# Token-block sums on VectorE alone, 1.6 setup steps per group, input matrices held for the later pairs

## The chip, the cores and the metric

The kernel runs on one core of a Trainium2 chip. The metric is the device time of one launch in microseconds (us). A core has TensorE (PE in the profile; its weight loads are PEld), VectorE (DVE), ScalarE (ACT), GpSimd (POOL) and SyncE (SP, which here issues all DMAs). Each engine runs its own instructions strictly in the order in which they stand, and waits on semaphores for the others.

## The reference

One layer of a hybrid encoder block over 768 tokens (512 of one request, 256 of another), width 1024, in float32:

```python
h = rms_norm(x, g_ffn1_pre)
x = x + 0.5 * rms_norm(swiglu(h, w_ffn1_gate, w_ffn1_up, w_ffn1_down), g_ffn1_post)
z = rms_norm(x, g_mix_pre) @ w_in          # -> u, q_c, kv_c, k_rope
y_ssm = rms_norm(s5_mixer(u, fwd, bwd, d_skip, w_glu, b_glu), g_ssm_out)
y_att = rms_norm(mla_mixer(q_c, kv_c, k_rope, g_q, w_uq, g_kv, w_ukv), g_att_out)
x = x + rms_norm(concat([y_ssm, y_att]) @ w_out, g_mix_post)
x = x + 0.5 * rms_norm(swiglu(rms_norm(x, g_ffn2_pre), w_ffn2_gate, w_ffn2_up, w_ffn2_down), g_ffn2_post)
```

`swiglu(x, g, u, d)` is `(silu(x @ g) * (x @ u)) @ d` with 2816 inner columns. The state-space mixer `s5_mixer` is a linear recurrence of 32 groups of 64 complex states in both directions. Its matrices depend on the weights alone, so the kernel works them out while the first feed-forward block (FFN1) runs.

## The kernel before

Every float32 operand of a matmul is split into a high and a low part (`split`, lines 97 to 99: a cast on ACT at L98, then a subtraction on DVE at L99), and each product is three matmuls: high by high (L117, L125), high by low (L118, L126), low by high (L119, L127). So ACT and DVE have to prepare every weight tile `w` before PE can use it.

A feed-forward block walks over 11 pairs of 256 inner columns (`ffn`). FFN1 does pairs 0 to 2 in the plain way (`plain`): eight groups of 24 matmuls of 384 columns each, four for gate and four for up, each group for one half of the tokens. From pair 3 on it uses a Strassen-Winograd form (`wino`) with seven products instead of eight. The form needs sums and differences of the four blocks B00, B01, B10, B11 of the normed tokens. `combos` makes them: four full blocks F (L266), three differences L280, L283, L285 and a fourth, L286, and then the split parts T1 to T4 (high on ACT at L271, low at L272). Each of these is one instruction over 128x1536 elements. In the kernel before, the sums of B11 and B10 (both L266), L286 and the low part T4l are on POOL, and the others on DVE. In the program's text `combos` is run beside the down products of pair 2 (FFN1) or of pair 0 (FFN2, which has one plain pair).

The down product of a pair (`down(q)`) is 12 groups of six matmuls of 512 columns (tile ps_d). In the first down product ACT copies each result to `acc` (L451); in the later ones DVE adds it (L453). A group can only start when one of two to four banks of ps_d has been read.

The state-space setup (`ssm_setup`, a generator of 99 steps) runs in the background of FFN1. After each group the call `behind(background, PACE[...])` adds a credit and runs as many steps as the credit allows, so that their instructions are written behind those of the group. The numbers of steps per group are 3.0 in pair 0, 1.15 in the other plain pairs and their down products, and 0.75 in the down products of the later pairs. The steps are, in order: 28 that build powers and factors; the way back (`ssm_back`, 22 steps), which transposes C (ps_c, L698) and then eight times makes two matrices on DVE (three instructions of 128x576 each, L679, L681 and L682, tiles ssm_w and ssm_t), multiplies them on PE (ps_k, L718, 16 small matmuls for each of the eight), and reads the two result banks on DVE (L726, L727) and ACT (L728, L729) into ssm_kf; then 48 steps for the 16 input matrices dM (L679 to L682 again, now of 128x512, on DVE; a transpose ps_m on PE; a copy on ACT; a DMA). The tiles ps_k have two banks, so one of the eight blocks can start on PE only when ssm_kf of the block before it has been read out.

The order within an engine is made by a scheduler from the text's order and the data each instruction needs; what it made of the two kernels is shown below where it matters.

Of the kernel before, what the change touches and what calls it, by code (L numbers as in the profile page):

```python
# [11 lines left out]
ALU = mybir.AluOpType  # L12
# [26 lines left out]
    return slice(HALF * i, HALF * i + HALF)  # L39


PACE = (3.0, 1.15, 0.75)
BACK = 27
WOUT = (35, 36, 37, 38)
AHEAD = 3
# [3 lines left out]
class Kernel:  # L49
    N6, N4, N2 = 20, 16, 4  # L50

    def __init__(self, tc, A, outs):
        self.tc, self.nc, self.A, self.outs = tc, tc.nc, A, outs
        self.credit, self.latest = 0, {}
        self.turns, self.free = [0, 0], False


    def s6(self, name, shape, dtype=F32):
# [202 lines left out]
    def combos(self, bl, out):  # L261

        def whole(kh, nh, eng):
            f = self.s6(f"F{kh}{nh}", [4, HALF])
            hi, lo = bl["B"][kh, nh]
            eng.tensor_tensor(f, hi.bitcast(F32), lo.bitcast(F32), op=ALU.add)  # L266
            return f

        def parts(name, src, eng):
            out[name] = h, l = tuple(self.s6(name + z, [4, HALF], F32R) for z in "hl")  # L270
            self.nc.scalar.copy(h, src)  # L271
            eng.tensor_tensor(l, src, h.bitcast(F32), op=ALU.subtract)  # L272

        dve, pool = self.nc.vector, self.nc.gpsimd
        b11 = whole(0, 0, dve)
        b22 = whole(1, 1, pool)
        yield
        b12 = whole(0, 1, dve)
        yield
        dve.tensor_tensor(b11, b12, b11, op=ALU.subtract)  # L280
        b21 = whole(1, 0, pool)
        yield
        dve.tensor_tensor(b12, b22, b12, op=ALU.subtract)  # L283
        yield
        dve.tensor_tensor(b22, b22, b11, op=ALU.subtract)  # L285
        pool.tensor_tensor(b21, b22, b21, op=ALU.subtract)  # L286
        yield
        parts("T2", b22, dve)
        yield
        parts("T1", b11, dve)  # L290
        yield
        parts("T3", b12, dve)
        parts("T4", b21, pool)
        yield

    def group(self, last, calls):
# [25 lines left out]
    def ffn(self, bl, wnames, way_out, n_plain, feed, lead, background=iter(()), read=lambda nh: None):  # L322
# [31 lines left out]
        def plain(q):  # L354
# [16 lines left out]
            for nh in range(2):  # L371
                for m in "gu":
                    for i in range(2):
                        if q == 0 and nh == 0:
                            next(feed, None)
                        with self.in_order() if q == 0 and nh == 0 else nullcontext():
                            if (m, i) not in ops:
                                get(m, i)
                            ps = self.gu([128, HALF])
                            for kh in range(2):  # L380
                                self.prod(ps, ops[m, i][kh], B[kh, nh], kh == 0, kh == 1)
                            if q == 0 and nh == 0 and m == "g":
                                get("u", i)
                            gate_done(hs, i, nh, ps) if m == "g" else up_done(hs, q, i, nh, ps)
                        if q or nh:
                            self.behind(background, PACE[1 if q else 0])

        def wino(m, q, T, hs, U):
# [69 lines left out]
        def down(q, side=background):  # L458
            product = row_of([q])[1]
            for t in range(NTILE):  # L460
                for dh in range(2):
                    product(t, dh, self.dn)()
                    if side is background:
                        self.behind(side, PACE[2 if q >= n_plain else 1])
                if side is not background:
                    next(side, None)
# [57 lines left out]
    def ssm_setup(self):  # L524
# [132 lines left out]
                yield  # L657
        yield from self.ssm_back(tB, PX)
        del tB, tC, tD, sm, PW, q, PX
        for b in range(16):  # L660
            w = self.s6("ssm_w", [3, 512])
            self.product(w[:, 0], w[:, 1], Bm, QW, 2 * b, 8)
# [620 lines left out]
```

## Time and profile before

| | |
|---|---|
| three runs | 1495.70, 1499.86, 1505.25 us; median 1499.86 us |
| profiled execution | 1495.48 us; its span from first to last instruction 1493.7 us |
| PE busy | 1410.8 us, 94% of the span |
| PEld, DVE, ACT, POOL busy | 87%, 67%, 38%, 18% |
| granted TensorE clock, mean | 0.981 |

All numbers of rows below come from the profiled execution; times in them count from the start of its span. A row of the timeline gives start, duration, engine, source line, operation, output and inputs, how often the instruction was repeated in a row, and in brackets the idle time of the engine before it with what ended it. A matmul is shown longer than it holds the engine, since matmuls overlap: the distance from one start to the next is what one costs. The same holds, by 0.05 to 0.08 us, for instructions on DVE.

### The profile page before, as it was taken

The numbers are of one execution on the slowest core, as the hardware profiler recorded it, in microseconds if no ns is written. First come the engines' busy times: TensorE is split into PE (matmuls) and PEld (weight loads), VectorE is DVE, ScalarE is ACT, GpSimd is POOL, SyncE is SP. The second block draws the span as 40 slices with busy tenths as digits, with TensorE's granted clock in tenths as the row PEclk, the third lists the DMA queues.
The fourth block names the chain that finished last, engine by engine and source line by source line (L and its number), as shares of the span: only waits on it lengthen the run. The fifth ranks groups of instructions, "written<-read, shape, count | busy, mean of one in ns | idle before, by whom it ended". The sixth has DMA issues, their size and how long they took to land. (4 is left out here: it accounts for less than half of the span.)

```text
span 1493.7 us, 20350 instructions
## 1 busy us (share of the span) xinstructions
PE 1410.8 (94%) x7868; PEld 1293.5 (87%) x7868; DVE 1006.9 (67%) x1614; ACT 574.5 (38%) x1085; POOL 263.4 (18%) x413
## 2 busy tenths in 40 slices
PE   6999779999999998899998899799999999999997
PEld 6989559999999997899877888598999999999995
DVE  5566898778887676624265545798777667776664
ACT  5331224223333242434764654346333222332231
POOL 1300110000000004203998112432000000000004
PEclk9999989999999999999999899899999999999999
DMA  9403412323213143553106334332221212212224
GB/s 240 88 14 99 147 36 87 104 71 106 79 64 99 57 130 95 167 163 98 22 14 165 90 102 148 120 104 81 71 71 57 85 57 73 83 53 75 72 84 113
DMA packets 116066, 137.51 MB, mean 92 GB/s; under 512 B 31745, under 2 KB 96641, under 8 KB 115969
## 3 DMA queue, kind: packets, MB, share of 16 engines
q1 hardware_dynamic: 115968, 136.21, 30.6%
q8 instruction: 62, 1.02, 0.3%
q14 instruction: 36, 0.29, 0.1%
HBM read 113.44 MB, written 21.95 MB: 91 GB/s over the span
## 5 line engine op out<-in xcount | busy, mean ns | idle before, releaser
L98 ACT CAST w<-raw 128x512 fp32r<-128x512 f32 (+3 forms) x327 | 219.5, 694 | 274.4 <-DVE raw L397 58.9
L99 DVE TENSOR_TENSOR w<-raw,w 128x512 fp32r<-128x512 f32 (+3 forms) x327 | 265.3, 823 | 56.7 <-ACT w L98 47.2
L453 DVE TENSOR_TENSOR acc<-acc,ps_d 128x512 f32<-128x512 f32 x216 | 146.5, 684 | 117.1 <-PE ps_d L127 117.0
L125 PE MATMUL ps_d<-w,hid 128*128 128x512 f32 x528 | 210.3, 399 | 11.4 <-DVE acc L453 6.2
L126 PE MATMUL ps_d<-w,hid 128*128 128x512 f32 x528 | 209.3, 396 | 2.0 <-DVE w L99 2.0
L127 PE MATMUL ps_d<-w,hid 128*128 128x512 f32 x528 | 208.1, 396 | 0.2 <-DVE hid L99 0.2
L1189 POOL TENSOR_SCALAR g<-g 128x1024 f32<-128x1024 f32 x2 | 5.6, 2778 | 738.6 <-DMA g<-in_g_ffn_post 414.4
L125 PEld LDWEIGHTS ps_d<-w,hid 128*128 128x128 f32 x528 | 100.3, 190 | 33.7 <-DVE acc L453 8.8
L127 PEld LDWEIGHTS ps_d<-w,hid 128*128 128x128 f32 x528 | 100.4, 190 | 22.3 <-DVE hid L99 0.6
L126 PEld LDWEIGHTS ps_d<-w,hid 128*128 128x128 f32 x528 | 100.4, 190 | 20.0 <-DVE w L99 2.5
L98 ACT CAST hid<-hs 128x384 fp32r<-128x384 f32 x88 | 44.3, 512 | 90.7 <-DVE hs L348 90.6
L400 ACT COPY U<-pa 128x384 f32<-128x384 f32 x36 | 17.2, 479 | 116.4 <-PE pa L119 111.4
L344 ACT ACTIVATE hs<-hs 128x384 f32<-128x384 f32 x54 | 27.7, 523 | 88.8 <-DVE hs L430 76.5
L99 DVE TENSOR_TENSOR hid<-hs,hid 128x384 fp32r<-128x384 f32 x88 | 47.9, 551 | 8.6 <-ACT hid L98 8.6
L118 PE MATMUL pb<-T2l,w 128*128 128x384 f32 x144 | 49.3, 342 | 2.9 <-DVE T2l L272 2.9
L119 PE MATMUL pa<-B00h,w 128*128 128x384 f32 x144 | 48.4, 336 | 0.8 <-DVE w L99 0.8
L119 PE MATMUL pb<-T2h,w 128*128 128x384 f32 x144 | 49.2, 342 | 0.0
L117 PE MATMUL pb<-T2h,w 128*128 128x384 f32 x144 | 48.9, 340 | 0.0
L994 DVE TENSOR_REDUCE mx<-ps_s 128x1 f32<-128x512 f32 (+1 forms) x40 | 27.2, 685 | 32.0 <-PE ps_s L991 32.0
L117 PE MATMUL pa<-B00h,w 128*128 128x384 f32 x144 | 48.3, 336 | 0.0
L117 PE MATMUL pe<-B11h,w 128*128 128x384 f32 x144 | 48.3, 336 | 0.0
L118 PE MATMUL pa<-B00l,w 128*128 128x384 f32 x144 | 48.3, 335 | 0.0
(367 smaller groups left out, 3769.8 us busy)
## 6 DMA issues: line engine op xcount, KB each, us to landing
raw<-in_w_ffn_gate SPq DMA_DIRECT2D x44, 512.0 KB, 4.6
raw<-in_w_ffn_up SPq DMA_DIRECT2D x44, 512.0 KB, 4.7
raw<-in_w_ffn_down SPq DMA_DIRECT2D x44, 512.0 KB, 3.9
x<-in_x_prompt SPq DMA_DIRECT2D x16, 256.0 KB, 8.0
dO<-ssm_w SPq DMA_DIRECT2D x16, 256.0 KB, 3.7
dM<-ssm_w SPq DMA_DIRECT2D x16, 256.0 KB, 2.0
raw<-dM SPq DMA_DIRECT2D x8, 512.0 KB, 5.7
raw<-dO SPq DMA_DIRECT2D x8, 512.0 KB, 3.8
```

The costliest lines, as they stand in the source:

```text
L98: self.nc.scalar.copy(hi, src)
L99: (eng or self.nc.vector).tensor_tensor(lo, src, hi.bitcast(F32), op=ALU.subtract)
L117: self.nc.tensor.matmul(ps, A[0][:, k, :], B[0][:, k, :], start=first, stop=False, skip_group_check=True)
L118: self.nc.tensor.matmul(ps, A[0][:, k, :], B[1][:, k, :], start=False, stop=False, skip_group_check=True)
L119: self.nc.tensor.matmul(ps, A[1][:, k, :], B[0][:, k, :], start=False, stop=stop and k == 3, skip_group_check=True)
L125: self.nc.tensor.matmul(ps, lh, rh, start=i == 0, stop=False)
L126: self.nc.tensor.matmul(ps, lh, rl, start=False, stop=False)
L127: self.nc.tensor.matmul(ps, ll, rh, start=False, stop=last)
L344: nc.scalar.activation(hs[:, i, half(nh)], ps, AF.Silu)
L400: nc.scalar.copy(U2, pa)
L453: tt(acc[:, t, sl], acc[:, t, sl], ps, op=ALU.add)
L994: nc.vector.tensor_reduce(m, ps, axis=AX.X, op=ALU.max)
```

## The change

Three edits. In `PACE` the second number goes from 1.15 to 1.6, so a plain group (and a group of a plain pair's down product) takes 1.6 setup steps with it. A flag `halfway` is set when `ssm_back` has ended; from then on only the down products of the later pairs run setup steps, so that of the dM matrices one is begun in the plain pairs and the rest comes with the later pairs. And in `combos` all instructions that were on POOL are on DVE.

```diff
-PACE = (3.0, 1.15, 0.75)
+PACE = (3.0, 1.6, 0.75)
...
-        self.turns, self.free = [0, 0], False
+        self.turns, self.free, self.halfway = [0, 0], False, False
...
-        dve, pool = self.nc.vector, self.nc.gpsimd
+        dve = self.nc.vector
         b11 = whole(0, 0, dve)
-        b22 = whole(1, 1, pool)
+        b22 = whole(1, 1, dve)
...
-        b21 = whole(1, 0, pool)
+        b21 = whole(1, 0, dve)
...
-        pool.tensor_tensor(b21, b22, b21, op=ALU.subtract)
+        dve.tensor_tensor(b21, b22, b21, op=ALU.subtract)
...
-        parts("T4", b21, pool)
+        parts("T4", b21, dve)
...
-                        if q or nh:
+                        if (q or nh) and not self.halfway:
                             self.behind(background, PACE[1 if q else 0])
...
-                    if side is background:
+                    if side is background and (q >= n_plain or not self.halfway):
                         self.behind(side, PACE[2 if q >= n_plain else 1])
...
         yield from self.ssm_back(tB, PX)
         del tB, tC, tD, sm, PW, q, PX
+        self.halfway = True
+        yield
```

After the change all lines behind the constructor of the class stand up to two lines lower (L679 is L681, L718 is L720, L726 is L728).

**PE, between the first down product and pair 2.** Before: the second and third rows of the down product's last group, one of the eight ps_k blocks (16 matmuls in the order, which the trace counts as 32), and then the gate products of pair 2 (ps from B00).

```order
L126 MATMUL ps_d<-w,hid 128x512
L127 MATMUL ps_d<-w,hid 128x512
L718 MATMUL ps_k<-ssm_w,ssm_b 32x128 x16
L117 MATMUL ps<-B00h,w 128x384
L118 MATMUL ps<-B00l,w 128x384
L117 MATMUL ps<-B00h,w 128x384
```

Now, at the same place:

```order
L126 MATMUL ps_d<-w,hid 128x512
L127 MATMUL ps_d<-w,hid 128x512
L720 MATMUL ps_k<-ssm_w,ssm_b 32x128 x64
L117 MATMUL ps<-B00h,w 128x384
L118 MATMUL ps<-B00l,w 128x384
L720 MATMUL ps_k<-ssm_w,ssm_b 32x128 x8
L117 MATMUL ps<-B00h,w 128x384
L118 MATMUL ps<-B00l,w 128x384
L117 MATMUL ps<-B00h,w 128x384
L118 MATMUL ps<-B00l,w 128x384
L720 MATMUL ps_k<-ssm_w,ssm_b 32x128 x8
L119 MATMUL ps<-B00h,w 128x384
```

Five of the eight ps_k blocks (64 and twice 8 matmuls) now stand ahead of the first low-part product (L119) of pair 2, where one stood. A first block stands further up, inside the down product (not shown), and ps_c stands behind 24 matmuls of the down product where it stood behind 48.

**DVE, the same place.** Before: the low parts `w` of pair 2's weights (L99) stand among the matrices of the way back.

```order
L681 TENSOR_TENSOR ssm_t<-ssm_ct,ssm_d 128x2x2x144
L99 TENSOR_TENSOR w<-raw,w 128x512 x2
L726 SCALAR_TENSOR_TENSOR ssm_kf<-mask,dsk,ps_k 128x16
L681 TENSOR_TENSOR ssm_t<-ssm_ct,ssm_d 128x2x2x144 x2
L682 TENSOR_TENSOR ssm_w<-ssm_w,ssm_t 128x576
L99 TENSOR_TENSOR w<-raw,w 128x512 x2
```

Now, where the first `w` of pair 2 stands:

```order
L729 TENSOR_TENSOR ssm_kf<-ssm_kf,ps_k 128x16
L684 TENSOR_TENSOR ssm_w<-ssm_w,ssm_t 128x576 x2
L728 SCALAR_TENSOR_TENSOR ssm_kf<-mask,dsk,ps_k 128x16
L681 TENSOR_TENSOR ssm_w<-ssm_ct,ssm_d 128x576
L683 TENSOR_TENSOR ssm_t<-ssm_ct,ssm_d 128x2x2x144
L681 TENSOR_TENSOR ssm_w<-ssm_ct,ssm_d 128x576
L683 TENSOR_TENSOR ssm_t<-ssm_ct,ssm_d 128x2x2x144
L729 TENSOR_TENSOR ssm_kf<-ssm_kf,ps_k 128x16
L99 TENSOR_TENSOR w<-raw,w 128x512 x2
L683 TENSOR_TENSOR ssm_t<-ssm_ct,ssm_d 128x2x2x144
L684 TENSOR_TENSOR ssm_w<-ssm_w,ssm_t 128x576
L99 TENSOR_TENSOR w<-raw,w 128x512 x2
```

From the first matrix to that first `w` DVE now has 40 instructions of 128x576 and ten small ones of ssm_kf; before, it had 11 of 128x576 there.

**DVE, the block sums of FFN1.** Before: the two sums that DVE had stand among the additions to `acc` of the down products of pairs 1 and 2, behind a part of a third dM matrix.

```order
L453 TENSOR_TENSOR acc<-acc,ps_d 128x512
L679 TENSOR_TENSOR ssm_w<-ssm_a 128x512
L681 TENSOR_TENSOR ssm_w<-ssm_a,ssm_q 128x2x2x128
L266 TENSOR_TENSOR F_1689<-B00h,B00l 128x1536
L266 TENSOR_TENSOR F_1709<-B01h,B01l 128x1536
L99 TENSOR_TENSOR w<-raw,w 128x512
L453 TENSOR_TENSOR acc<-acc,ps_d 128x512 x2
```

Now all four stand ahead of the first addition to `acc`, behind the only dM matrix that is begun in the plain pairs:

```order
L681 TENSOR_TENSOR ssm_w<-ssm_a 128x512
L683 TENSOR_TENSOR ssm_w<-ssm_a,ssm_q 128x2x2x128
L266 TENSOR_TENSOR F_1667<-B00h,B00l 128x1536
L266 TENSOR_TENSOR F_1669<-B11h,B11l 128x1536
L266 TENSOR_TENSOR F_1687<-B01h,B01l 128x1536
L266 TENSOR_TENSOR F_1706<-B10h,B10l 128x1536
L396 TENSOR_TENSOR raw<-raw 128x4x128 x2
L684 TENSOR_TENSOR ssm_w<-ssm_w 128x512
L99 TENSOR_TENSOR w<-raw,w 128x1024
L280 TENSOR_TENSOR F_1667<-F_1687,F_1667 128x1536
L348 TENSOR_TENSOR hs<-hs,ps 128x384
```

The four sums moved up, ahead of the last `hs` of pair 2 (L348), while PE still has pair 2's products to do. On PE the 24 groups of the two down products, which stood mostly ahead of pair 3's products, now alternate with them; behind pair 3 both orders hold the same work.

## Rows read from the trace of the kernel before

**Rows 1.** The page: busy share in 40 slices of 37.3 us, in tenths.

```profile
PE   6999779999999998899998899799999999999997
DVE  5566898778887676624265545798777667776664
```

**Rows 2.** Busy time (times instructions) by stage: PE, PEld, DVE, ACT, POOL, PEclk, DMA, GB/s.

```profile
91.06:150.00 58.94, 55.82 (x428) 49.86 (x428) 35.83 (x65) 18.11 (x38) 0.00 (x0) 0.97 0.29 72
150.00:225.00 75.00, 54.90 (x299) 41.77 (x299) 69.35 (x87) 20.61 (x33) 14.91 (x4) 0.91 0.30 91
225.00:244.94 19.94, 19.94 (x114) 19.53 (x114) 15.85 (x26) 8.12 (x15) 0.00 (x0) 1.00 0.42 137
...
244.94:545.00 300.06, 300.06 (x1607) 280.89 (x1607) 234.88 (x389) 106.21 (x188) 0.00 (x0) 1.00 0.24 77
...
1000.00:1025.00 25.00, 22.53 (x111) 19.66 (x110) 24.31 (x26) 14.15 (x22) 8.79 (x2) 1.00 0.14 43
```

**Rows 3.** Timeline of PE: what matmuls cost, and where the stage stalls.

```profile
99.94 0.39 PE L125 MATMUL ps_d<-w,hid 128*128 128x512 f32 x1
100.62 0.39 PE L125 MATMUL ps_d<-w,hid 128*128 128x512 f32 x1
101.99 1.03 PE L698 MATMUL ps_c<-ident,craw 128*128 128x128 f32 x8
112.25 0.69 PE L119 MATMUL ps<-B00h,w 128*128 128x384 f32 x1 [0.93 <-DVE w L99]
115.62 0.37 PE L117 MATMUL ps<-B10h,w 128*128 128x384 f32 x1
117.75 0.33 PE L117 MATMUL ps<-B00h,w 128*128 128x384 f32 x1
118.27 0.33 PE L117 MATMUL ps<-B00h,w 128*128 128x384 f32 x1
167.84 0.64 PE L718 MATMUL ps_k<-ssm_w,ssm_b 64*32 64x128 f32 x16 [2.71 <-ACT ssm_kf L729]
202.48 0.79 PE L125 MATMUL ps_d<-w,hid 128*128 128x512 f32 x1 [4.68 <-DVE acc L453]
218.15 0.69 PE L118 MATMUL pb<-T2l,w 128*128 128x384 f32 x1 [2.85 <-DVE T2l L272]
244.94 0.33 PE L117 MATMUL pa<-B00h,w 128*128 128x384 f32 x1
```

**Rows 4.** Timeline of DVE: the way back, weights, additions, block sums.

```profile
103.78 0.76 DVE L679 TENSOR_TENSOR ssm_w<-ssm_ct,ssm_d 128x576 f32<-128x576 f32 x1 [10.07 <-ACT ssm_ct L699]
105.92 0.75 DVE L679 TENSOR_TENSOR ssm_w<-ssm_ct,ssm_d 128x576 f32<-128x576 f32 x1
114.87 1.28 DVE L99 TENSOR_TENSOR w<-raw,w 128x512 fp32r<-128x512 f32 x2
197.21 1.75 DVE L266 TENSOR_TENSOR F<-B00h,B00l 128x1536 f32<-128x1536 f32 x1
198.88 1.75 DVE L266 TENSOR_TENSOR F<-B01h,B01l 128x1536 f32<-128x1536 f32 x1
201.15 1.27 DVE L453 TENSOR_TENSOR acc<-acc,ps_d 128x512 f32<-128x512 f32 x2
```

**Rows 5.** Timeline of POOL and DVE: the same kinds of instruction beside POOL and alone.

```profile
173.99 3.51 POOL L266 TENSOR_TENSOR F<-B10h,B10l 128x1536 f32<-128x1536 f32 x1 [1.75 <-DVE w L99]
...
174.59 3.46 DVE L395 TENSOR_TENSOR s<-raw 128x512 f32<-128x512 f32 x1
179.77 0.68 DVE L395 TENSOR_TENSOR s<-raw 128x512 f32<-128x512 f32 x1
...
1007.78 3.52 POOL L286 TENSOR_TENSOR F<-F,F 128x1536 f32<-128x1536 f32 x1 [12.38 <-DVE F L285]
...
1008.03 3.82 DVE L99 TENSOR_TENSOR w<-raw,w 128x512 fp32r<-128x512 f32 x1
...
1017.42 0.50 PE L125 MATMUL ps_d<-w,hid 128*128 128x512 f32 x1 [2.47 <-ACT acc L451]
```

## The prediction

> **What bounds the kernel now.** I read the page's slices first: PE is at 9 tenths nearly everywhere, and among the four dips below 8 tenths lies one in slices 5 and 6 (187 to 224 us), where DVE stands at 8 and 7 [rows 1]. So the kernel is bound by PE, and only time in which PE stands still or runs slowly can be won. Then I cut FFN1 into stages [rows 2]. From 91.06 us (first down product) to 150 PE idles 3.1 us of 58.9. From 150 to 225 it idles 20.1 us of 75, and DVE is busy 69.35 of them: there PE waits for DVE. From 225 PE is never idle, up to 545. The granted clock is 0.97 and 0.91 in the first two stages and 1.00 in the other two; 1.00 is 2.4 GHz, and one step below is 1.2 GHz, so a mean of 0.91 over 75 us is 13.5 us at the lower level, of which half is lost. That is the price of the stalls on top of the idle time. The timeline names the stalls: an addition to acc that comes late on DVE (4.68 us at 202.48), the low part of T2 (2.85 at 218.15), a ps_k block behind ssm_kf (2.71 at 167.84) [rows 3]. A row to hold the change against: at 244.94 PE begins the first product of pair 4's gate [rows 3]. Up to there both orders put the same work on PE, but for two of the dM transposes ps_m, which now come later (of the order of 0.55 us each, by ps_c's eight in 1.03 [rows 3]).
>
> **Prices.** Three matmuls of a down group start every 100.62 - 99.94 = 0.68 us, so a group of six costs 1.36 and 24 of them 32.6. Three of 384 columns cost 118.27 - 117.75 = 0.52, so pair 2's 192 cost 33.3 and the 156 of pair 3 up to pair 4's first cost 27.0 [rows 3]. A matrix of the way back (three instructions) costs DVE 105.92 - 103.78 = 2.14, or 0.71 each; a w of 512 columns 0.60 to 0.64 (two in 1.28); an addition the same (two in 1.27); an instruction of 1536 columns 198.88 - 197.21 = 1.67 [rows 4]. So the work of PE from 91.06 to 244.94 is 36 groups 49.0, ps_c 1.0, eight ps_k blocks of 0.65 5.2, pair 2 33.3, pair 3 27.0, two ps_m 1.1: 116.6 of 153.9. The other 37.3 are idle time, slow clock and restarts; this is what the change can win at most in FFN1.
>
> **Edit 1, 1.6 steps: the way back comes earlier and in one block.** ps_c moves up by 24 matmuls, 5.4 us, from 101.99 to 96.6. DVE had then waited 10.07 us for it [rows 3, 4]. It can't use all 5.4: part of the factor work now stands behind the last hs of pair 1, and I let the first matrix start at 100 instead of 103.78. Ahead of the first w of pair 2 stand 40 instructions of the way back, 40 x 0.71 = 28.4, and ten small ones of ssm_kf, 1.5 together by an estimate of 0.15 each (their rows are not costed singly): DVE reaches that w at 130, and PE has its low part at 130.7. Meanwhile PE has eight groups left in the down product, 10.9 us from 97.6, about 1 us of waiting for the first block of ps_k, and six blocks of 0.65: it runs dry at about 111 and idles some 16.5 us up to 130.7. This is the new wait, and all of pair 2 is queued behind it, on PE in the same order. It takes the place of the 3.1 us before 150. From 130.7: 190 matmuls, 33.0, two blocks 1.3, and 1.7 because PE restarts slowly (before, after its stalls, ten matmuls took 115.62 - 112.25 = 3.4 us, twice their 1.7 [rows 3]). PE ends pair 2 at 166.7.
>
> What this buys: the way back is done when pair 2 begins, and through these 36 us DVE has only pair 2's own work, two of the eight blocks and the four sums F, which need nothing of pair 2. I take the two down products and pair 3, 32.6 + 27.0 = 59.6 us of PE, and walk the two orders against each other by these prices: PE waits for an addition behind a 1.67 us instruction at five places and for T3's low part once, 0.2 to 1.6 us each, together 4.5. Pair 4 begins at 166.7 + 59.6 + 4.5 = 230.8, which is 14.1 earlier than 244.94; some 24 of the 37.3 stay lost. Bounds: if each handover ps_k to ssm_kf to the next ps_k takes 1.5 us more in five rounds (a wait of 2.71 for one stands in [rows 3]), the block costs 7.5 more; if the first matrix starts at 98.4, 1.6 less. The 4.5 lie between 0 and 10.2, which the three stalls at 167.84, 202.48 and 218.15 alone cost now [rows 3]; I am near the low end, since the F rows now stand in time that PE fills with pair 2.
>
> **Edit 2, dM held.** Two dM matrices with their products (3 x 0.64 = 1.9 us of DVE each) go from the plain pairs to the later ones: their DVE time is in the sum above, since they are out of the walked rows. In the later pairs PE is busy 300.06 of 300.06 us and DVE 234.9 [rows 2]; the rate there stays 0.75 steps a group, and 47 steps need 63 of 72 groups, so none is left for the end. Their price is the PE time alone, 2 x 0.55 = 1.1 us. If DVE were no cover there, it would be 3.8 more. The dM transfers also stay behind the copies in SP's queue; weights behind them are loaded a pair ahead. Zero for that, at most 1.
>
> **Edit 3, no POOL.** DVE takes four more instructions of 1.67 in each feed-forward block, 6.7 us. But it doesn't lose that: beside a POOL instruction of 3.51 us a DVE instruction took 3.46 that takes 0.68 alone, and beside one of 3.52 another took 3.82 [rows 5]. These two lost 2.78 and 3.14 us (the w of 512 columns 0.68 alone, too). I take 2.5 for each of the four, 10 in each block, so DVE gains about 3 there; the bounds are 2 and 3.2 each. In FFN1 this is in the walk, which uses the prices of instructions alone. In FFN2 PE loses only 2.47 us near 1017, an addition on ACT that is late behind a weight DVE had not finished [rows 2, 5]; I take 2 of it, between 0 and 2.5.
>
> The Trainium skill, SBUF — State Buffer, section "SBUF: two separate sides", calls the port pair of the two engines an exclusive lock: who comes second is blocked for the whole instruction. The rows agree in kind (3.46 beside 3.51), but by the rule DVE would lose all of POOL's 14.9 us in FFN1 [rows 2], where the two rows lose 2.8 and 3.1 of 3.5; the sum would come out up to 5 us lower, 1479.
>
> **Sum.** FFN1: 14.1 - 1.1 = 13.0, less 2 for a further dip of the clock among the short waits at 175 to 190, as an estimate (in the stage from 150 the clock costs 6.7 us): 11. FFN2: 2. Together 13, against the execution's own 1495.48: 1482.5. The median of the runs, 1499.86, lies 4.4 above that execution, so a run at the median would come to 1487; I say 1484.
>
> **Rivals.**
> *The wait only moves (no change).* The 16.5 us on PE are real, and of the 20.1 us that PE idles from 150 to 225 [rows 2] more than 9 stay, because T2 to T4 still have to be made between additions. Then FFN1 gives 0 to 6, the total 2 to 8: 1490. For it: DVE's work up to pair 4 hardly shrinks, and DVE was busy 69 of 75 us. Against it: it was idle 23 of 58.9 us before 150, and that is the time now used.
> *Slower.* The handovers of the five blocks are as long as before, 7.5 us more, and DVE comes to pair 2's end so late that all 20.1 us stay: 16.5 + 7.5 - 3.1 = 21 lost, 1.1 for dM: 1495.5 + 22 - 2 = 1515. It is slower as soon as more than about 12 of the 20.1 stay: the block costs 13.4 net, and each idle us of that stage brings half as much again in slow clock and restarts. Against it: four F sums and both L395 stand ahead of the first addition now.
> *More.* The five short waits vanish (4.5), the clock stays at 2.4 GHz behind 134 (2), FFN2 gives 2.5: 13 + 7 = 20, 1476.
> *Clock.* PE idles long at 111 to 131; should it stay at 1.2 GHz through pair 2's first half, that is 8 us more: 1491. The rows have it back after 3.4 us, so this is in the first rival's share.
> The Trainium skill, TensorE: Matmul & The Clock Gate, Part 1, has the array's clock fall to half when it is idle and come back under load. The row from 112.25 shows that for a short stall; no run here shows it for 16 us.
>
> **How the numbers follow.** My case, a gain of 8 to 17 us: 0.52. The wait moves: 0.27. More: 0.14. Slower: 0.07. The range 1474 to 1497 holds my case with both ends of its unknown terms, most of the second, and half of the third, with some 4 us of spread between runs. About 1% (15 us) is what a measurement of this kernel can tell from no change. Faster by over that: "more" and the top two fifths of mine, 0.34; slower 0.07; the rest, 0.59, is within it.
>
> **What would show it.** ps_c near 96.6 and the first matrix near 100; a PE gap of some 16 us ending near 131 on DVE's first w of pair 2; PE idle below 6 us from there to pair 4, which begins near 231; no DVE row above 3 us; PE full in the later pairs, DVE about 4 us busier there; no wait of 2.47 in FFN2. Wrong if the gap is over 22 us, or if waits for acc and T2 over 10 us remain behind it.

## The result, and the profile after

Four runs of the changed kernel took 1478.53 to 1480.35 us, median 1479.79; four runs of the kernel before, beside them, 1495.70 to 1505.87, median 1502.55. The ratio is 0.9871, with a 95% interval of 0.9848 to 0.9894: 1.29% faster. A second set gave 1477.67 against 1496.79, 0.9867 (0.9847 to 0.9886). The profiled execution took 1479.79 us, 15.7 less than the 1495.48 of before; the prediction's sum for this pair was 13.0.

The page of the changed kernel, busy tenths in 40 slices (here of 36.95 us), answers to [rows 1]:

```profile
PE   6998999999999997999997999799999999999997
DVE  5578977877878666525164635797687666776764
```

The dip of slices 5 and 6 is gone from PE's row; one digit of 8 stands in slice 4, where the way back of the state-space setup now lies. By stage (columns as in [rows 2]), from the first down product at 92.07 us on, and in FFN2:

```profile
92.07:150.00 57.93, 50.79 (x439) 40.54 (x439) 49.09 (x86) 19.43 (x43) 0.00 (x0) 0.85 0.53 143
150.00:225.00 75.00, 72.29 (x367) 64.99 (x366) 63.78 (x84) 22.83 (x36) 0.00 (x0) 1.00 0.18 58
...
229.82:530.00 300.18, 300.18 (x1612) 281.38 (x1612) 237.09 (x398) 108.67 (x191) 0.00 (x0) 1.00 0.26 81
...
985.00:1010.00 25.00, 25.00 (x126) 22.56 (x126) 24.72 (x28) 15.25 (x23) 0.00 (x0) 1.00 0.16 43
```

Ahead of 150 us PE now idles 7.1 us where it idled 3.1, at a mean clock of 0.85 where it was 0.97. From 150 to 225 it idles 2.7 where it idled 20.1, and the clock is 1.00 where it was 0.91. The later pairs are full as before, and in FFN2 the idle 2.5 us are gone. The timeline of PE shows the places, answering to [rows 3]:

```profile
97.56 1.03 PE L700 MATMUL ps_c<-ident,craw 128*128 128x128 f32 x8
114.67 0.64 PE L720 MATMUL ps_k<-ssm_w,ssm_b 64*32 64x128 f32 x16 [1.82 <-ACT ssm_kf L730]
116.76 1.08 PE L720 MATMUL ps_k<-ssm_w,ssm_b 64*32 64x128 f32 x16 [1.45 <-ACT ssm_kf L731]
124.61 1.08 PE L720 MATMUL ps_k<-ssm_w,ssm_b 64*32 64x128 f32 x16 [1.68 <-ACT ssm_kf L731]
125.61 0.69 PE L117 MATMUL ps<-B00h,w 128*128 128x384 f32 x1
130.14 0.69 PE L119 MATMUL ps<-B00h,w 128*128 128x384 f32 x1
165.70 0.39 PE L125 MATMUL ps_d<-w,hid 128*128 128x512 f32 x1
180.91 0.50 PE L125 MATMUL ps_d<-w,hid 128*128 128x512 f32 x1 [1.21 <-DVE acc L453]
188.91 0.44 PE L118 MATMUL pc<-T3l,w 128*128 128x384 f32 x1 [1.21 <-DVE T3l L272]
229.82 0.33 PE L117 MATMUL pa<-B00h,w 128*128 128x384 f32 x1
```

The idle time ahead of 126 lies in the handovers between one ps_k block and the next (a block can start when ssm_kf of an earlier one has been read out). Pair 2 begins at 125.61 with its high parts and gets its first low part at 130.14; it ends at 165.70, where the next down product starts. Behind it two waits of 1.21 us remain for an addition and for T3's low part. Pair 4 begins at 229.82, where it began at 244.94: 15.12 us earlier. On DVE, answering to [rows 4]:

```profile
100.25 0.76 DVE L681 TENSOR_TENSOR ssm_w<-ssm_ct,ssm_d 128x576 f32<-128x576 f32 x1 [0.26 <-ACT ssm_ct L701]
128.41 1.30 DVE L99 TENSOR_TENSOR w<-raw,w 128x512 fp32r<-128x512 f32 x2
154.63 1.75 DVE L266 TENSOR_TENSOR F<-B00h,B00l 128x1536 f32<-128x1536 f32 x1
159.63 1.76 DVE L266 TENSOR_TENSOR F<-B10h,B10l 128x1536 f32<-128x1536 f32 x1
```

The 40 instructions of the way back and the small ones among them run from 100.25 to 128.41 without a hole, and the four block sums from 154.63 on, while PE still works on pair 2.

### The profile page after: what moved, and what is told of

Its sections match the earlier page's. It is cut to its first block, busy times and chain, and to the rows that moved or that the text cites. A ratio compares the mean times of both kernels' runs of the same rounds, so it can differ in the third digit from the quotient of the medians.

```text
span 1478.0 us, 20330 instructions
## 1 busy us (share of the span) xinstructions
PE 1410.6 (95%) x7868; PEld 1295.5 (88%) x7868; DVE 994.9 (67%) x1622; ACT 575.1 (39%) x1085; POOL 229.5 (16%) x405
## 5 line engine op out<-in xcount | busy, mean ns | idle before, releaser
L99 DVE TENSOR_TENSOR w<-raw,w 128x512 fp32r<-128x512 f32 (+3 forms) x327 | 252.4, 783 | 58.3 <-ACT w L98 48.2
L395 DVE TENSOR_TENSOR s<-raw 128x512 f32<-128x512 f32 x36 | 24.8, 692 | 42.7 <-DMA raw<-in_w_ffn_up 35.6
L99 DVE TENSOR_TENSOR hid<-hs,hid 128x384 fp32r<-128x384 f32 x88 | 48.8, 556 | 7.0 <-ACT hid L98 7.0
L118 PE MATMUL pc<-T3l,w 128*128 128x384 f32 x144 | 48.2, 335 | 1.2 <-DVE T3l L272 1.2
L119 PE MATMUL pb<-T2h,w 128*128 128x384 f32 x144 | 48.3, 336 | 0.0
L119 PE MATMUL pa<-B00h,w 128*128 128x384 f32 x144 | 48.3, 336 | 0.0
```

The costliest lines, as they stand in the source:

```text
L99: (eng or self.nc.vector).tensor_tensor(lo, src, hi.bitcast(F32), op=ALU.subtract)
L118: self.nc.tensor.matmul(ps, A[0][:, k, :], B[1][:, k, :], start=False, stop=False, skip_group_check=True)
L119: self.nc.tensor.matmul(ps, A[1][:, k, :], B[0][:, k, :], start=False, stop=stop and k == 3, skip_group_check=True)
L395: tt(s1, a21, a22, op=ALU.add)
```

## The experiments

Each kernel is read at three distances in its profile, all between starts on PE: from the first down product to pair 4's gate (FFN1's critical stretch); from pair 1 to pair 2 of FFN2 (where `combos` runs there); and from the first attention product ps_s to pair 1 of FFN2, where all kernels have the same code. Ratios are to the kernel before, in the same set of runs, with 95% intervals. Of the eight combinations of the three edits two were not run: the steps with the sums but without the hold, and the hold with the sums but without the steps.

| kernel | down product to pair 4 | pair 1 to 2, FFN2 | ps_s to pair 1, FFN2 | median, us | ratio |
|---|---|---|---|---|---|
| before, first and second profile | 153.88, 153.60 | 40.92, 41.35 | 268.3, 267.4 | 1496.8 to 1502.6 | 1 |
| 1.6 steps alone | 170.48 | 41.37 | 267.9 | 1511.98 | 1.0107 (1.0088 to 1.0125) |
| hold alone | 147.72 | 42.49 | 272.8 | 1497.29 | 0.9986 (0.9968 to 1.0004) |
| sums on DVE alone | 151.47 | 38.18 | 267.4 | 1493.77 | 0.9971 (0.9958 to 0.9984) |
| 1.6 steps and hold | 136.70 | 41.37 | 269.9 | 1481.20 | 0.9896 (0.9881 to 0.9910) |
| same, sums on DVE in FFN2 only | 136.68 | 38.19 | 272.5 | 1481.15 | 0.9887 (0.9863 to 0.9911) |
| changed (all three), two profiles | 137.75, 137.22 | 38.18, 38.19 | 268.5, 268.5 | 1479.79, 1477.67 | 0.9871, 0.9867 |
| changed, 1.4 steps | 140.73 | 38.18 | 268.0 | 1483.98 | 0.9895 (0.9871 to 0.9918) |
| changed, 4.5 and 1.6 | 130.81* | 38.18 | 272.7 | 1481.73 | 0.9890 (0.9861 to 0.9920) |
| changed, 5.0 and 1.45 | 131.36* | 38.18 | 272.3 | 1479.50 | 0.9875 (0.9854 to 0.9897) |
| changed, 5.0 and 1.6 | 129.29 | 38.19 | 273.1 | 1476.21 | 0.9830 (0.9798 to 0.9862) |
| changed, 7.0 and 1.0 | 120.68* | 38.19 | 268.4 | 1485.73 | 0.9908 (0.9884 to 0.9932) |

(*) Not the same work: in these three, 204 matmuls ps_d stand ahead of pair 4's begin, in all others 216. The other 12, two groups of 1.36 us, come later, so 2.7 us of these distances are only moved.

**One edit at a time: 1.6 steps alone.**

```diff
-PACE = (3.0, 1.15, 0.75)
+PACE = (3.0, 1.6, 0.75)
```

> Edit 1 without edits 2 and 3: 1.6 steps per plain group, dM not held, POOL kept. In the order about ten more dM matrices come ahead of T1 to T4 than before (some 30 instructions of 0.64 us, 19 us of DVE). Theory of the prediction (DVE's time up to pair 4 sets the end): the block pays only with the hold; pair 4, at 244.94 us in before and 229.82 in the changed kernel, begins between 238 and 250, and the kernel is within 1% of before. Rival (the early block is the whole gain and dM matrices fit into DVE's idle time): pair 4 begins near 232, and the kernel is 10 us or more faster.

Pair 4 begins at 263.28, later than either theory had it, and the kernel is 13 us slower than before. Without the hold the faster steps run on into the dM matrices in the plain pairs. The busy time of ps_m from the first down product to pair 4 (columns as in [rows 2], without DVE and POOL), in the kernel before and in this one, counts them: four transposes each, so two matrices before and nine here.

```profile
91.06:244.94 153.88, 1.26 (x8) 0.92 (x8) 1.18 (x2) 0.94 0.31 90
```

```profile
92.80:263.28 170.48, 6.62 (x36) 4.60 (x36) 5.29 (x9) 0.89 0.31 91
```

The waits of PE in the whole execution name what I had not priced: these transposes stand in PE's queue ahead of products and wait for DVE. The first row is from the view of waits (us in total, times, longest), the other two from the timeline.

```profile
PE ps_m L666 <- DVE ssm_w L682: 18.4, 5, 7.6
```

```profile
204.90 0.68 PE L666 MATMUL ps_m<-ident,ssm_w 128*128 128x128 f32 x4 [4.44 <-DVE ssm_w L682]
220.94 1.08 PE L666 MATMUL ps_m<-ident,ssm_w 128*128 128x128 f32 x4 [7.57 <-DVE ssm_w L682]
```

**The sums on DVE alone** (the part of the diff in `combos`).

> Edit 3 alone: the block sums on DVE, 1.15 steps, dM not held. Theory of the prediction (a POOL instruction costs DVE about 2.5 us, a DVE one of the same work 1.67): DVE gains some 3 us in FFN1 and 2 to 2.7 in FFN2; pair 4 begins near 242, the whole is 5 us faster. Rival (exclusive use of the port pair: DVE loses all of POOL's 14.9 us in FFN1 and gets 6.7 back): pair 4 begins near 237, the whole is 10 us faster. Rival (edit 3 does nothing where the wait lies): pair 4 stays at 244 to 246. Of the spread: before ran between 1495.7 and 1505.9, the changed kernel between 1478.5 and 1480.4; if POOL beside DVE makes that spread, this kernel is free of it.

The distance to pair 4 falls by 2.4 us and that in FFN2 by 2.7, 5.1 in the medians: about the two gains that the prediction gave to edit 3 (3 and 2), and half of what exclusive use of the port pair would have given. DVE's busy time from the first down product to pair 4 falls from 121.03 to 118.04 us, the 3 of the walk. The stall that the addition makes got longer (4.68 in [rows 3]), since all four sums now stand ahead of it; what fell away are waits around it, such as the 2.85 for T2l:

```profile
201.85 0.79 PE L125 MATMUL ps_d<-w,hid 128*128 128x512 f32 x1 [8.02 <-DVE acc L453]
242.56 0.33 PE L117 MATMUL pa<-B00h,w 128*128 128x384 f32 x1
```

**The hold alone** (`halfway` as in the change, 1.15 steps, POOL kept).

> Edit 2 alone: dM held for the later pairs, 1.15 steps, POOL kept. Theory of the prediction: two dM matrices of 1.9 us each leave DVE's stretch ahead of pair 4, and 1.1 us of PE time is moved: pair 4 begins 3 to 5 us earlier, near 241, and the whole is 2 to 4 us faster. Rival (the four sums, which the scheduler can now put earlier, are what is late): pair 4 begins near 235 and the whole is 8 us or more faster. Rival (the way back itself is what is late): no change of pair 4's begin.

FFN1's stretch falls by 6.2 us, between my 3 to 5 and the rival's 10, but the whole by 1.6 in the median. The 1.6 are not clear of the noise: the interval of the ratio holds 1. In this profile 2.7 of the 6.2 are gone between pair 10 and the start of the last down product of FFN1, nearly all of it in one wait of 2.44 us for pc on DVE (more on it below), 4.5 in the stretch up to FFN2, where the code is the same (below), and 1.6 in FFN2.

**1.6 steps and hold, POOL kept.**

> The changed kernel without edit 3: 1.6 steps, dM held, POOL kept for its four instructions. Theory of the prediction: FFN1 loses about 3 us of DVE time, of which part is hidden, so pair 4 begins at 230 to 233, and FFN2 loses 2.7; the whole is 3 to 6 us slower than the changed kernel (1479.8). Rival (exclusive use of the port pair): pair 4 begins near 238, the whole is 10 us slower than the changed kernel. If this kernel spreads over 10 us as before does, POOL beside DVE makes the spread; if it is as steady as the changed kernel, the long waits behind 150 us do.

Pair 4 comes 136.7 us behind the first down product, 1 us less than with the sums on DVE. So edit 3 brings nothing in FFN1 once the other two are in, against the 3 us of my theory. The whole is 1.4 us slower than the changed kernel by the medians of two sets and some 4 by the two ratios, whose intervals overlap, so it says little on the 3 to 6 expected. POOL's timeline fits: its two block sums now start at 138 and 146, where DVE has room (busy 16.26 of the 22 us from 130 to 152) and PE is never idle. DVE does lose time to the first of them, 3.98 us for a w that takes 1.23 alone, but PE doesn't have to wait for it.

```profile
137.93 4.55 POOL L266 TENSOR_TENSOR F<-B11h,B11l 128x1536 f32<-128x1536 f32 x1 [74.10 <-ACT ssm_kf L731]
145.97 3.80 POOL L266 TENSOR_TENSOR F<-B10h,B10l 128x1536 f32<-128x1536 f32 x1 [3.49 <-PE ps_k L720]
```

```profile
139.57 3.98 DVE L99 TENSOR_TENSOR w<-raw,w 128x1024 fp32r<-128x1024 f32 x1 [0.45 <-ACT w L98]
```

```profile
130.00:152.00 22.00, 22.00 (x181) 20.73 (x170) 16.26 (x25) 6.79 (x14) 8.35 (x2) 0.90 0.60 175
```

Taken with the two single edits this is the main finding: in one set of runs the steps cost 13.1 us, the hold gains 1.6, and both together gain 17.7. The sum of the single effects would be a loss of 11.5; 29 us come from the combination. The gain of the hold alone is not clear of the noise; the other two are.

**The sums on DVE in FFN2 alone**, with edits 1 and 2, to place edit 3's gain.

```diff
-        dve = self.nc.vector
+        dve, pool = self.nc.vector, self.nc.vector if lone else self.nc.gpsimd
```

(`lone` is set for FFN2; the four instructions are issued through `pool` again.)

> Edits 1 and 2, and edit 3 in FFN2 alone: in FFN1 POOL keeps its four instructions. Theory formed from the runs so far (in FFN1 POOL's two sums run at 138 and 146 us, where DVE waits anyway, so edit 3 is worth nothing there; in FFN2 it is worth 2.7 to 4.3): pair 4 of FFN1 begins at 229 as in the kernel with POOL in both, pair 1 to pair 2 of FFN2 takes 38.2 us as in the changed kernel, the whole is within 2 us of the changed kernel. Rival (the prediction's 3 us of edit 3 in FFN1, or more by exclusive use of the port pair): 3 to 7 us slower than the changed kernel.

FFN1 is as with POOL in both (136.68), FFN2 as in the changed kernel (38.19): edit 3 works in FFN2, and there alone. The whole missed my 2 us: 1481.15 is 3.5 us above the changed kernel's 1477.67 in the same set, within the rival's 3 to 7, though the two intervals overlap. The rival's reason is not in the trace: both stretches are as the theory said, and in the profiles the difference lies in the third distance (272.5 against 268.5), where the code is the same. Over the five profiles that keep POOL in FFN2 its distance is 40.9 to 42.5, over the nine others 38.18 or 38.19, so the edit's worth there is 2.7 to 3.2 us, and 4.3 against the hold alone, where the granted clock also falls there, from 1020.1 to 1023.5.

**How early the way back should come.** Five kernels change the steps of the changed one.

```diff
-PACE = (3.0, 1.6, 0.75)
+PACE = (7.0, 1.0, 0.75)
```

The others have 5.0 and 1.6, 5.0 and 1.45, 4.5 and 1.6, 3.0 and 1.4 as their first two numbers.

> The changed kernel with 7.0 and 1.0 steps in place of 3.0 and 1.6: the way back begins after 120 instead of 264 plain products behind pair 0, and its ps_k blocks stand one by one between groups of pair 1, of the down product and of pair 2, where the changed kernel has 64 and 2 x 8 in one place. From the first down product to pair 3 the changed kernel takes 76.8 us for some 56 us of PE work. Theory of the prediction (PE's gap behind the down product is the price of the block, DVE has room earlier: it is busy 49.6 of the first 92 us): some 10 to 16 us of it come back, the kernel runs at 1464 to 1472. Rival (DVE's 40 instructions only move the wait into pair 1, whose weights come late): 1476 to 1490.

The rival holds, for the most part with a single wait: the way back stands ahead of pair 1's weights on DVE, and PE waits 10 us for the first low part, in 12.6 us of idle time from 60 to 92. The clock is at its lower level from 71.5 to 81.8, and ps_c and two of the eight blocks now lie ahead of the down product too. The first down product comes 18.4 us later than in the changed kernel, and the stretch behind it, 17 us shorter, doesn't quite give that back; at pair 6 the kernel is 5.5 us behind the changed one.

```profile
78.59 0.69 PE L119 MATMUL ps<-B00h,w 128*128 128x384 f32 x1 [10.09 <-DVE w L99]
```

> The changed kernel with 5.0 steps in pair 0 in place of 3.0, and 1.6 as it is: ps_c stands ahead of the last 24 products of pair 1, the block behind the down product shrinks from 64 + 8 + 8 to 48 small matmuls. Theory of the prediction: the way back begins some 9 us earlier, PE's gap behind the down product shrinks by 4 to 8 us, the kernel runs at 1471 to 1476. Rival (the wait moves into pair 1): 1478 to 1484.

This one did nearly as my theory said (1476.21 is just above its 1471 to 1476): the gap shrinks, to some 2.9 us of waits between blocks where the changed kernel has 6.9, at the price of 4.3 us at the first down product, whose weights are late now (rows below). Pair 4 begins at 223.51, 6.3 earlier than in the changed kernel. The median, 1476.21, is the lowest of all, but the two were timed in different sets and their intervals overlap (0.9798 to 0.9862 here, 0.9847 to 0.9886 in the changed kernel's second set), so that it beats the changed kernel is likely and not shown.

```profile
94.22 0.72 PE L125 MATMUL ps_d<-w,hid 128*128 128x512 f32 x2 [2.14 <-ACT w L98]
97.13 0.80 PE L126 MATMUL ps_d<-w,hid 128*128 128x512 f32 x1 [2.19 <-DVE w L99]
```

> 5.0 and 1.45 steps in place of 3.0 and 1.6. The way back begins as early as with 5.0 and 1.6 (pair 4 at 223.5 us there), with one more group between its blocks, so DVE comes to the weights of the first down product sooner (they were 4.3 us late there). Theory (the room that counts is DVE's between pair 1 and pair 2): pair 4 begins at 221 to 224, the whole 1472 to 1476. Rival (the way back then ends too late for the block sums, as with 1.4): pair 4 near 228, 1478 to 1482.

> 4.5 steps in pair 0 in place of 3.0, and 1.6 as it is: ps_c stands at the very start of the first down product (24 matmuls earlier than in the changed kernel, behind pair 1's products), and 56 small matmuls stand in the block behind it, where the changed kernel has 64. Theory: nothing of pair 1 is delayed, the way back begins 5 us earlier, and pair 4 begins at 224 to 227; the whole 1474 to 1478. Rival (the handovers of the 56 keep the gap as it is): pair 4 at 229, 1479 to 1481.

Both theories missed in the time: 1479.50 is in the rival's range, 1481.73 above both ranges. Both begin pair 4 early (226.57, later than my 221 to 224, and 223.91, a little earlier than my 224 to 227), but 2.7 us of that are two down groups that come later (the note to the table). In the second PE also waits 2.2 us at the first down product for a weight from ACT, which the theory had left out. From pair 6 of FFN1 to the first ps_s they fall back by 9.2 and 8.3 us against the first profile of before, where the changed kernel falls back by 2.5 and the one with 5.0 and 1.6 by 3.0. Of the 6.7 and 5.8 us between them and the changed kernel 2.7 are the two down groups, and 3.1 and 3.2 a wait in the last pair for pc, which DVE does behind a w that waits for ACT. The row is from the first of the two:

```profile
545.78 0.45 PE L117 MATMUL pe<-B11h,w 128*128 128x384 f32 x1 [3.09 <-DVE pc L423]
```

This wait, 1.5 to 3.2 us long, stands in the five profiles in which no dM matrix was begun ahead of pair 4 (the hold alone; 7.0 and 1.0; 5.0 and 1.45; 4.5; 1.4) and in none of the nine others; in the changed kernel one is begun. So to hold back all sixteen goes with a price at the end of FFN1; why was not tested.

> The changed kernel with 1.4 steps in place of 1.6: the first w of pair 2 stands behind fewer matrices of the way back, but the way back ends within pair 2, and half of the four sums come behind it, among the first additions to acc. Theory of the prediction (what counts is that the way back and the sums are over when the additions begin; the gap ahead of pair 2 costs less than the waits behind it): 3 to 8 us slower than the changed kernel, 1483 to 1488. Rival (the gap is the larger loss): 3 to 6 us faster, 1474 to 1477.

With 1.4 steps the stretch is 3 us longer and the kernel 4 to 6 slower than the changed one, as the theory had it: what counts is that way back and sums are over when the additions to acc begin. PE idles 12.1 us of the stretch where it idles 9.9 in the changed kernel, and from 150 to 225 the mean clock is 0.95 and not 1.00.

**Where the runs spread.** The kernel before ran between 1494.9 and 1505.9 us, which is more than some of the terms above, so it was profiled again.

> The kernel before, unchanged, profiled once more, to see where its spread between runs lies (1494.9 to 1505.9 in 27 runs, while the changed kernel's four lie in 1.8 us). Theory 1 (the long waits between 150 and 225 us make it): the time from the first down product to pair 4, 153.9 us in the first profile, differs by several us. Theory 2 (POOL beside DVE in the second feed-forward block): the time from pair 1 to pair 2 there, 40.92 us in the first profile and 38.18 with the sums on DVE, differs by 1 to 2 us. Theory 3 (the parts between the feed-forward blocks, where the code is the same in all kernels): the time from pair 10 of FFN1 to the first product of pair 1 in FFN2, 485.6 us in the first profile, differs by several us; then the spread has nothing to do with the change.

FFN1's stretch is the same within 0.3 us, FFN2's within 0.4: theories 1 and 2 find nothing in these two profiles. Both are of executions at the low end of the spread (1495.48 and 1494.16 us), so what a long run of before loses was not profiled. The third distance is what differs from profile to profile, with two groups, 267.4 to 269.9 and 272.3 to 273.1, whatever was edited. The granted clock goes with it. Below is the same code in the two cases, in windows of 4 us of the output product of the mixers (columns as in [rows 2]): the kernel before, first profile, then the one with the hold alone.

```profile
916.00:920.00 4.00, 3.45 (x17) 2.54 (x15) 3.21 (x4) 2.53 (x6) 1.84 (x2) 1.00 0.01 5
920.00:924.00 4.00, 3.75 (x22) 2.95 (x21) 1.76 (x5) 0.71 (x2) 1.24 (x1) 1.00 0.02 4
924.00:928.00 4.00, 4.00 (x19) 3.29 (x18) 1.50 (x2) 1.15 (x2) 0.63 (x3) 1.00 0.00 0
```

```profile
916.00:920.00 4.00, 3.33 (x13) 1.84 (x11) 3.21 (x6) 2.53 (x5) 0.95 (x2) 1.00 0.00 0
920.00:924.00 4.00, 3.87 (x17) 3.52 (x18) 1.27 (x4) 0.00 (x0) 1.34 (x1) 0.63 0.02 4
924.00:928.00 4.00, 4.00 (x11) 3.04 (x10) 1.04 (x2) 0.00 (x0) 0.00 (x0) 0.51 0.00 0
```

In both PE waits 0.55 and 0.19 us and then runs twelve matmuls of one column, which the timelines of the two show as

```profile
921.01 1.47 PE L167 MATMUL ps_r<-ones,Sv 128*128 128x1 f32 x12 [0.19 <-DVE Sv L1155]
```

```profile
920.13 1.83 PE L167 MATMUL ps_r<-ones,Sv 128*128 128x1 f32 x12 [0.19 <-DVE Sv L1157]
```

Behind that the clock stays at 1.00 in one and falls to 0.51 in the other, where eleven matmuls pass in 4 us and not nineteen. In the 30 us around this place the mean clock is 0.89 in the five profiles of the long group and 0.94 to 1.00 in the nine others. A mean of 0.89 is some 6.8 us at half speed, which costs at most 3.4 of the 4.6 us between the two groups' means; the rest was not traced.

The mean clock of whole runs points the same way. In the 23 runs of the kernel before beside the first four experiments it is 0.978 to 0.983 in the six below 1497 us and 0.976 to 0.978 in the five above 1502. Between the two means, 0.981 and 0.977, lie some 12 us at the lower level, so up to 6 of the 8 us between their times. Where in those runs the clock fell is not known.

> The changed kernel itself in more runs. If the spread lies in the parts between the feed-forward blocks, as the second profile of the kernel before says (from the first ps_s to pair 1 of FFN2: 268.3 and 267.4 us there, 272.8 and 273.1 in two kernels with the same code in this stretch), the four runs within 1.8 us were chance: more runs of it spread over 4 us or more. If the long waits of FFN1 made the spread of before, it stays within 2 us. Median by the four runs 1479.8, ratio 0.987.

The eight runs of the changed kernel lie between 1476.9 and 1480.4. The new four spread by 3.4 us, between the 4 or more and the 2 that I had set, so neither reading is shown. Some kernels spread as little (1.6 steps and hold: 3.6 us in four runs), others more (5.0 and 1.6: 8.5), and both profiles of the changed kernel are of the short group. Whether that is chance or this kernel's timing stays open.

## Why the prediction was right, and where it was off

The time of 1484 us was 4.2 too high, with the measured one inside its range; the outcome, faster by over 1%, had got 0.34, and "within 1%" 0.59. The mechanism held: PE's stalls behind 150 us went, at the price of a new gap ahead of pair 2. Most terms came out a little better than said, and two things agree by luck in part (below).

**Where FFN1 loses.** Right. The stalls from 150 to 225 went from 20.1 to 2.7 us; of the 37.3 us that could be won 22.2 stay lost (137.75 of stretch less 115.5 of work), where the prediction said some 24.

**The way back moved up.** ps_c was to gain 5.4 us: it stands 5.49 behind the first down product, 10.93 before. The first matrix was put at 100 and came at 100.25, DVE was to reach the first w of pair 2 at 130 and reached it at 128.41, since 28.16 us held the whole row: starts of 128x576 instructions are 0.67 apart on the whole, where I had 0.71. (All times of this profile stand some 1.0 us late by its start: the first down product begins at 92.07, not 91.06.)

**The new gap.** Right in place and cause (PE dry at 111.95, said 111; first low-part product at 130.14, said 130.7). Its make-up was different: PE doesn't stand idle for 16.5 us. It is idle 6.9 between 111.95 and 125.61, works through the blocks, and from 125.61 multiplies by the high parts, which don't wait for DVE's subtraction. From 116.5 to 133.5 the clock is at its lower level of 1.2 GHz.

```profile
117.00:121.00 4.00, 2.29 (x33) 1.13 (x26) 4.00 (x9) 0.50 (x2) 0.00 (x0) 0.50 0.35 84
125.61:130.14 4.53, 4.53 (x42) 2.81 (x38) 4.53 (x9) 2.06 (x5) 0.00 (x0) 0.50 0.96 314
130.14:134.00 3.86, 3.86 (x17) 3.86 (x14) 3.86 (x8) 1.82 (x3) 0.00 (x0) 0.56 0.29 90
134.00:139.44 5.44, 5.44 (x33) 5.44 (x32) 4.99 (x10) 1.84 (x4) 0.00 (x0) 1.00 0.72 162
```

The 1.7 us that I put for a slow restart behind the first low part came out: ten products take 3.4 us from 130.14 to 133.51, against 10 x 0.173 = 1.7 at the upper level. Ahead of it the slow clock costs little more. The first of the two w of the row at 128.41 was ready at about 129.05, and PE, at work on half a block at the lower level, came to it at 130.14. By this estimate the clock costs 2.7 us at most; the rival "clock" had asked for 8. The Trainium skill, TensorE: Matmul & The Clock Gate, Part 1, has the array at half clock after idling until it has been busy again for some time; the rows agree, since PE was idle 3.5 of the 4.8 us ahead of the block at 116.76 and has not been idle since 125.61 when the clock is back. Over the whole stretch the clock is down no less than before: 0.15 of 57.93 us is 17 us at the lower level, and [rows 2] has 0.03 of 58.94 and 0.09 of 75, also 17 us. What changed is that most of it now lies where PE waits for DVE anyway. The low parts begin 0.6 us earlier than said, with four more high products (0.7) done ahead of them, and pair 2 ends at 165.70 where 166.7 was said.

**Pair 2 to pair 4.** The sum is right to the tenth: 59.6 + 4.5 = 64.1 us said, 229.82 - 165.70 = 64.12 measured. That is luck in part. The waits came to 2.7 of the 4.5, and the products and down groups kept PE busy for 61.4 us where my prices gave 59.6; the two errors cancel.

**The sum against the profiles**, all from starts on PE in the two first profiles:

| term | said | measured |
|---|---|---|
| pair 4 begins earlier | 14.1 | 15.12 (15.64 at pair 6) |
| dM in the later pairs | -1.1 | -1.26 from pair 6 to pair 10 |
| a further dip of the clock in FFN1 | -2 | 0, the clock is 1.00 from 150 to 225 |
| end of FFN1 up to ps_s | none | -1.19 |
| ps_s to FFN2 | none | -0.23 |
| FFN2 | 2 | 2.74 |
| sum | 13.0 | 15.7 |

From its own first down product the changed kernel comes to pair 4 16.1 us sooner (153.88 against 137.75); the 15.12 hold 1.0 us that it begins later, and such starts differ by 1.7 us between two profiles of one kernel (91.06 and 89.38 before). The 1.19 at the end of FFN1 is within what two profiles of one kernel differ by: from pair 10 to ps_s the kernel before takes 217.3 and 218.4 us, the changed one 218.5 and 218.0.

The step that was mis-sized is the dip of the clock: 2 us for the short waits behind 175, which came to 2.7 us of idle time with the clock at 1.00 throughout. These are 2 of the 2.7 by which the sum was short. Of the rest, FFN1 and FFN2 gave 1.5 and 0.7 more than said, and the end of FFN1, of which I had said nothing, took 1.2 back.

**From the sum to the time.** The other 1.5 us are the way from 1482.5 to 1484, a guess at the spread between runs that had taken the profile of before as fast by 4.4. The profile of the changed kernel is at its own median. That gap also makes the result look larger than the work saved: 22.8 us between the medians of the first set and 19.1 in the second, where the profiles differ by 15.7. Since FFN1's stretch of before is the same in two profiles, the rest is in the spread of the kernel before, for which the profiles and the runs' mean clocks point at the granted clock (above); no long run of it was profiled. The chance for "faster" was too low because I worked it out from sums against a fast execution, and counted the median half.

**Edit 2 at the price of 1.1 us only.** Right for its cost, wrong for its worth. I booked two dM matrices leaving the stretch. With 1.6 steps and no hold nine of the sixteen come into it, and the same steps lose 13 us; the hold keeps out all but the one that is begun. The comparison that I had made was with the order of before, and there it does little (1.6 us, not clear of the noise). DVE was to be some 4 us busier in the later pairs; the two rows of 300 us have 2.2 (237.09 against 234.88 in [rows 2]).

**Edit 3.** 3 us in FFN1 by the walk were wrong in company: 2.4 alone, nothing beside edits 1 and 2, since POOL's sums then lie in time that DVE has to spare. FFN2 came out better than said (2.74 against the first profile of before, 2 said, 2.5 at most). By the rule that I took from the Trainium skill, SBUF — State Buffer, section "SBUF: two separate sides", the time would be 1479 (1484 less 5; my sum of 1482.5 less 5 is 1477.5). That is near the measured one, but not for its reason: the 5 us were to come from FFN1, and there the kernel that keeps POOL is no slower. That DVE would lose all of POOL's time was my reading of it: an instruction that comes in the middle is blocked only for the rest. The lock itself is as that section says (below).

**The rivals.** "The wait only moves" needed more than 9 of the 20.1 us to stay; 2.7 did. "Slower" needed the handovers to cost as much as before (2.71 for one in [rows 3]) and all stalls to stay; the blocks waited 0.3 to 1.8 us each. "More" had part of its reasons right: the clock stayed up behind 134 as it asked, and FFN2 gave all. But the short waits shrank only from 4.5 to 2.7, and its 20 us lie further from the 15.7 of the two profiles than my 13.

## What to carry to other kernels

A step rate and a rule on what those steps may contain are one change: test them together and each alone, because here one alone loses 13 us, the other alone gains 1.6, which is not clear of the noise, and both gain 17.7. When helper work has to pass through a queue that PE waits on, put it in one block just ahead of the stretch where that queue is busiest, and not so early that it stands ahead of the weights of an earlier stage: here 5.0 steps in pair 0 (with 1.6 behind) were as good as 3.0 or better, and 7.0 (with 1.0 behind) 6 us slower. Price work moved off an engine only where that engine is late, and compare a sum made against one profile with the kernel's median over runs only after looking at what makes the runs differ.

## What the runs showed of the hardware

**After the same short pause the clock may fall or not.** In the same code, behind 0.7 us of idle time in two pieces and twelve one-column matmuls, the granted clock fell to its lower level for some 6.8 us in five profiles out of fourteen, for half as long in one, and not in eight; the stretch was 272.3 to 273.1 us long in the five, 269.9 in the one and 267.4 to 268.5 in the eight.

**What POOL blocks on DVE.** From the kernel before, timeline of POOL and DVE in FFN1:

```profile
168.65 3.59 POOL L266 TENSOR_TENSOR F<-B11h,B11l 128x1536 f32<-128x1536 f32 x1 [106.05 <-PE ps_k L718]
...
167.66 1.23 DVE L99 TENSOR_TENSOR w<-raw,w 128x1024 fp32r<-128x1024 f32 x1 [0.83 <-ACT w L98]
168.80 0.68 DVE L453 TENSOR_TENSOR acc<-acc,ps_d 128x512 f32<-128x512 f32 x1
169.40 0.17 DVE L727 TENSOR_TENSOR ssm_kf<-ssm_kf,ps_k 128x16 f32<-128x16 f32 x1
169.48 4.44 DVE L99 TENSOR_TENSOR w<-raw,w 128x1024 fp32r<-128x1024 f32 x2
```

The last row merges two instructions. The view that keeps shapes apart, in a window of these rows, has them singly; the first is

```profile
L99 DVE TENSOR_TENSOR w<-raw,w 128x1024 fp32r<-128x1024 f32 x1 | 3.8, 3842 | 0.0
```

The addition, one of whose inputs is a PSUM bank, takes its usual 0.68 us beside POOL; the next instruction with two SBUF inputs waits until POOL is done: 3.84 us where the same shape took 1.23 at 167.66, so 2.6 lost, with 2.8 left of POOL's when it began. The two rows of [rows 5] lost 2.8 and 3.1 with 2.9 and 3.3 left. So an instruction on POOL costs DVE only what is left of it when DVE reaches such an instruction. It works the other way too: in FFN2 of before the T4l on POOL, 4.30 us in FFN1, took 7.92 from 1019.73 on, beside six DVE instructions that follow each other without a gap. The Trainium skill has such a lock in SBUF — State Buffer, "SBUF: two separate sides": whichever of the two starts first has the port pair for its whole instruction, and on DVE's side an instruction with two SBUF inputs takes part. The trace agrees, with 3.84 beside POOL for 1.23 alone.
